# A decoder trunk on one core: x loaded turned and split by features, the value convolution's additions moved into accumulating DMAs, and another order of the DeltaNet groups

## The chip, the cores and the metric

The kernel runs on one core of a Trainium2 chip. The metric is the device time of one execution in microseconds (us); lower is better. The kernel before was timed at a median of 2768.34 us over three runs (2768.11 to 2770.29). One further execution was profiled; it took 2768.12 us, and its trace spans 2766.0 us from the first instruction to the last. The five engines work from queues of their own, each in the order of its queue: PE (TensorE) multiplies matrices, DVE (VectorE) and ACT (ScalarE) work on vectors, POOL (GpSimd) does small vector work and issues DMAs, SP (SyncE) only issues DMAs here.

## The reference

Two layers over 256 tokens of 2048 features. Each has a token mixer and a SwiGLU feed-forward network, each of these behind an RMSNorm and with a residual addition; a last RMSNorm follows.

```
h = x
h = h + gdn_mixer(rmsnorm(h), ...)      # gated DeltaNet, 16 key heads, 32 value heads
h = h + swiglu(rmsnorm(h), ...)
h = h + hgrn2_mixer(rmsnorm(h), ...)
h = h + swiglu(rmsnorm(h), ...)
return rmsnorm(h)
```

All of it is float32. What this change touches is the DeltaNet mixer and the normalization ahead of it:

```
proj = rmsnorm(x) @ w_in                       # k, q, v, z and the gates b, a
qkv  = silu(causal_depthwise_conv(qkv, conv))  # four taps along the tokens
o    = gated_delta_rule_chunked(q, k, v, beta, g)   # chunks of 64 tokens, one 64x64 inverse each
o    = rmsnorm(o) * silu(z)
return o @ w_out
```

rmsnorm divides each token by the root of its mean square. The kernel multiplies the raw x by the norm's weights only and applies the token's factor, called `rstd`, to the products.

## The kernel before

**Weights.** Every weight matrix is streamed once. A "half" is a tile of 128 by 1024 floats (512 KB): SP loads it into one of four buffers `raw`, ACT rounds it to `wh`, DVE forms the rest `wl = raw - wh`, and PE multiplies `wh` with the rounded and the remaining part of the activations (`xt_h`, `xt_l`) and `wl` with the rounded part: three products for one, which keep float32 accuracy. `wh` and `wl` have four buffers each. Results gather in two PSUM tiles called `main`. There are 945 halves.

**Groups.** The halves that make one result tile form a group. In the DeltaNet mixer there is one group for the gates (`ba`, one half, 48 products), and for each of eight head groups (hg) one for keys and queries (k0 to k7, eight halves, 192 products of 256 columns), one for the values (v0 to v7) and one for the output gate (z0 to z7), both of eight halves with 96 products of 512 columns; four output projections o0 to o3 (16 halves each) take the results of two head groups each. `GDN_ORDER` gives the order in which PE works them off; `ba` goes first.

**The start.** `setup` and `start` load the identity and norm weights (`head`) and x in four tiles of 128 tokens by 2 by 512 features (`first0`, `first1`, `x`, `x`), all on the SP queue; ten matmuls of ones warm PE up. PE turns x by 32 transposes into PSUM (`make_xt`), ACT and DVE split what comes out into `xt_h` and `xt_l` (`split_scaled`), and ACT squares and sums x for `rstd` (`sumsq`).

**Between the groups.** When k of a head group is done, `conv_evac` multiplies it by the tokens' factors (`rstd_row`) out of PSUM, `gdn_qk` does the convolution, the decay matrices `dec` and the matrices `nmat`, and `gdn_inverse` inverts: the rows go through DRAM (`n_dram`) into the tile `wide`, 31 pairs of short DVE operations on `u` solve the small blocks, a round trip through DRAM spreads them (`um`, shown as `u`), and PE and ACT join them. When v is done, `gdn_v` copies it into `r`, writes it to DRAM, and reads it back three times shifted by one to three tokens (tile `before`, one buffer); DVE multiplies by the tap's weights and adds to `r`. When z is done, `gdn_o` combines inverse, values and scores and `head_out` gives `ot_h` and `ot_l`, the operands of the output projection. `nmat`, `dec`, `r` and `zs` have two buffers, `wide`, `u` and `before` one.

**Order on the engines.** All operations are first recorded. A planner (`Recorder.plan`) then runs through them with an estimated cost of each and a due time counted back from the products on PE, and fixes every engine's queue; POOL's DMAs are planned with 0.75 us to issue and 6.5 us to land. On the chip each queue runs strictly in that order. Since one helper issues everything, nearly all rows of the profile carry the line L490; groups are told apart by tile.

Of the kernel before, what the change touches and what calls it, by code (L numbers as in the profile page):

```python
# [33 lines left out]
    "k0 k1 k2 k3 v0 v1 z0 z1 v2 k4 z2 k5 v3 z3 k6 v4 o0 k7 v5 v6 z4 o1 z5 z6 v7 z7 o2 o3"  # L34
# [472 lines left out]
class Trunk:  # L507
# [27 lines left out]
    def setup(self):  # L535
# [3 lines left out]
        self.x_at, self.x = self.a["x"], {}  # L539
        head = t([P, P + 64], "head")  # L540
        nc.sync.dma_start(head, self.a["head"])
        nc.ops[-1].lag = 2.4
        self.queue = [nc.ops[-1]]
        self.ident = head[:, 0:P]
        self.norms = head[:, P : P + 64].rearrange("p (n c) -> p n c", n=4)
        self.ones = t([P, P], "ones")
        nc.gpsimd.memset(self.ones, 1.0)
        self.neghalf = t([P, 8], "neghalf")
        nc.gpsimd.memset(self.neghalf, -0.5)
        self.rstd = t([P, 2], "rstd")  # L550
        self.rstdh = t([P, 2], "rstdh")
        self.rstd_row = t([P, T], "rstd_row")
        self.ssp = t([P, 2, 4], "ssp")
        self.ss = t([P, 2], "ss")
        self.junk = t([P, 512], "junk")
        self.vjunk = t([P, 256], "vjunk")
# [3 lines left out]
    def start(self, norm, row):  # L560

        pool = self.nc.pool("first", 1, phase=True)
        for cg in range(4):
            if cg < 2:
                self.x[cg] = self.tile(pool, [P, 2, 512], f"first{cg}")
            else:
                self.x[cg] = self.tile(self.xpool, [P, 2, 512], "x", ordered=True)
            self.nc.sync.dma_start(self.x[cg], self.x_cols(self.x_at, cg))
            self.nc.ops[-1].lag = (2.5, 2.2, 3.0, 3.0)[cg]
            self.nc.edge(self.queue[-1], self.nc.ops[-1])  # L570
            self.queue.append(self.nc.ops[-1])
        warm = self.aux()
        for i in range(10):
            self.nc.tensor.matmul(
                warm[:, (i % 4) * P : (i % 4 + 1) * P], self.ones, self.ones, start=True, stop=True
            )
        for cg in range(4):
            self.make_xt(cg, norm)
        for cg in range(4):
            self.nc.after(self.xt_h[cg])  # L580
            self.sumsq(cg)
        self.nc.close(pool)
        self.make_rstd(row)
# [3 lines left out]
    def stream(self, groups):  # L587
# [10 lines left out]
        def load(n):  # L598
            g, i = flat[n]
            raw = self.tile(self.wraw, [P, 1024], "raw", ordered=True)  # L600
            nc.sync.dma_start(raw, g.halves[i])
            if n == 0:
                nc.ops[-1].lag = 4.2
                nc.edge(self.queue[1], nc.ops[-1])
            h = place("wh", g)
            nc.scalar.activation(h, raw, AF.Copy)
            low = place("wl", g)
            nc.vector.tensor_tensor(out=low, in0=raw, in1=h.bitcast(F32), op=ALU.subtract)
            ready[n] = (h, low)
# [42 lines left out]
    def mm_cols(self, ps, i, wh, wl, n_k, n_f, n_chunks):  # L652

        for k in range(n_k):
            kt = i * n_k + k
            xh, xl = self.operand(kt)
            for f in range(n_f):
                at = (k * n_f + f) * P
                for m, (w, s) in enumerate(((wh, xh), (wh, xl), (wl, xh))):
                    self.nc.tensor.matmul(  # L660
                        ps[:, f // 2, (f % 2) * T : (f % 2 + 1) * T], w[:, at : at + P], s,
                        start=(kt == 0 and m == 0 and f % 2 == 0),
                        stop=(i == 2 * n_chunks - 1 and k == n_k - 1 and m == 2),
                        skip_group_check=True,
                    )
# [616 lines left out]
    def gdn(self, after):  # L1282
# [4 lines left out]
        def gates_end(ps):  # L1287
            self.gdn_gates(ps)
# [472 lines left out]
```

## Time and profile before

| what | value |
|---|---|
| median of three runs | 2768.34 us |
| profiled execution | 2768.12 us |
| its span | 2766.0 us |
| PE busy | 99% of the span |
| weight loads of PE | 84% |
| DVE busy | 69% |
| ACT busy | 52% |
| POOL busy | 9% |
| HBM | 209 GB/s over the span |

The page counts for each engine the time in which one of its instructions runs. A row of a timeline gives the start in us from the span's begin, the duration, engine, line, operation, the tiles written and read, the shapes and the count; in square brackets stands how long the engine was idle before it and what ended that. A matmul's duration is longer than its distance to the next one, as matmuls overlap; the distance is what costs time.

### The profile page before, as it was taken

To read this page: it belongs to the slowest core of one execution; us is meant where nothing else is said; L and a number is where in the kernel's file an instruction comes from. 1 tells how busy PE (TensorE), PEld (TensorE's weight loads), DVE (VectorE), ACT (ScalarE), POOL (GpSimd) and SP (SyncE) were. 2 spreads that over 40 slices of the span, in tenths; PEclk is the share of its full clock that TensorE was granted. 3 is DMA by queue.
4 is the path that set the end of the run, shared out by engine and by line. 5 is a ranking of instruction groups with operands and counts; after the bars stand their busy time and mean duration, and the time that the engine had idled before them with its cause. 6 is when DMAs were issued, how large, how long until landed. Compare 5 with 4: busy or idle time off the path is not lost.

```text
span 2766.0 us, 41091 instructions
## 1 busy us (share of the span) xinstructions
PE 2749.6 (99%) x15662; PEld 2333.5 (84%) x15662; DVE 1899.9 (69%) x2857; ACT 1428.6 (52%) x2010; POOL 251.6 (9%) x370
## 2 busy tenths in 40 slices
PE   9999999999999999999999999999999999999998
PEld 9888888888888888888888989988888888888887
DVE  7787888877766667446675688778657675456764
ACT  6646666565554444344444556556454444344443
POOL 1213222232110000000000100000100000000000
PEclk9999999999999999999999999999999999999999
DMA  7686668687776666676667655555776666766664
GB/s 262 201 282 222 189 213 286 205 276 218 229 254 202 193 194 194 224 223 195 192 191 224 219 163 175 168 166 176 231 258 195 193 193 209 224 208 194 195 200 160
DMA packets 162677, 580.52 MB, mean 210 GB/s; under 512 B 20138, under 2 KB 21306, under 8 KB 162352
## 3 DMA queue, kind: packets, MB, share of 16 engines
q1 hardware_dynamic: 138912, 503.15, 57.0%
q0 software_dynamic: 23280, 73.91, 8.5%
q8 instruction: 122, 2.00, 0.3%
q10 hardware_dynamic: 288, 0.85, 0.1%
q14 instruction: 75, 0.61, 0.1%
HBM read 550.52 MB, written 27.31 MB: 209 GB/s over the span
## 4 chain that ended last, share of the span: by engine, by line
PE 99%; ACT 0%; DVE 0%; issue 0%; DMA 0%; SPq 0%; POOLq 0%; POOL 0%; ACTq 0%
PE main L490 92%; PE aux L490 6%; ACT dec L490 0%; DMA first<-in_x 0%; DVE wl L490 0%; ACT wh L490 0%; DVE utmp L490 0%; SPq L490 0%; DVE pre L490 0%; ACT xt_h L490 0%; DVE u L490 0%; ACT y L490 0%; POOLq L1757 0%; ACT junk L490 0%; DVE xl L490 0%
## 5 line engine op out<-in xcount | busy, mean ns | idle before, releaser
L490 DVE TENSOR_TENSOR wl<-raw,wh 128x1024 fp32r<-128x1024 f32 x945 | 1160.7, 1229 | 755.6 <-ACT wh L490 742.2
L490 ACT ACTIVATE wh<-raw 128x1024 fp32r<-128x1024 f32 x945 | 1000.8, 1060 | 1226.9 <-PE main L490 1126.3
L490 PE MATMUL main<-wh,xt_h 128*128 128x512 f32 x2176 | 849.3, 390 | 0.8 <-ACT wh L490 0.8
L490 PE MATMUL main<-wl,xt_h 128*128 128x512 f32 x2176 | 848.4, 390 | 1.3 <-DVE wl L490 1.3
L490 PE MATMUL main<-wh,xt_l 128*128 128x512 f32 x2176 | 849.5, 390 | 0.0
L490 PEld LDWEIGHTS main<-wl,xt_h 128*128 128x128 f32 x2176 | 408.5, 188 | 85.7 <-DVE wl L490 1.6
L490 PEld LDWEIGHTS main<-wh,xt_h 128*128 128x128 f32 x2176 | 408.5, 188 | 85.0 <-ACT wh L490 1.2
L490 PEld LDWEIGHTS main<-wh,xt_l 128*128 128x128 f32 x2176 | 408.6, 188 | 84.4
L490 PE MATMUL main<-xt_h,wh 128*128 128x256 f32 (+1 forms) x1040 | 290.5, 279 | 0.7 <-ACT wh L490 0.7
L490 PE MATMUL main<-xt_h,wl 128*128 128x256 f32 (+1 forms) x1040 | 290.1, 279 | 1.0 <-DVE wl L490 0.9
L490 PE MATMUL main<-xt_l,wh 128*128 128x256 f32 (+1 forms) x1040 | 290.0, 279 | 0.3 <-DVE xt_l L490 0.3
L490 PE MATMUL main<-wh,htl 128*128 128x512 f32 x664 | 258.6, 389 | 0.0
L490 PE MATMUL main<-wl,hth 128*128 128x512 f32 x664 | 258.3, 389 | 0.0
L490 PE MATMUL main<-wh,hth 128*128 128x512 f32 x664 | 258.3, 389 | 0.0
L490 PEld LDWEIGHTS main<-xt_h,wl 128*128 128x128 f32 (+1 forms) x1040 | 194.5, 187 | 1.5 <-DVE wl L490 1.4
L490 PEld LDWEIGHTS main<-xt_h,wh 128*128 128x128 f32 (+1 forms) x1040 | 194.5, 187 | 1.3 <-ACT wh L490 0.9
L490 PEld LDWEIGHTS main<-xt_l,wh 128*128 128x128 f32 (+1 forms) x1040 | 194.5, 187 | 1.0 <-DVE xt_l L490 0.5
L490 DVE STREAM_TRANSPOSE turned<-h 32x256 f32<-32x256 f32 x352 | 153.5, 436 | 7.2
L490 PE MATMUL main<-wh,ot_l 128*128 128x512 f32 x384 | 151.2, 394 | 0.0
L490 PE MATMUL main<-wh,ot_h 128*128 128x512 f32 x384 | 150.6, 392 | 0.0
L490 PE MATMUL main<-wl,ot_h 128*128 128x512 f32 x384 | 150.5, 392 | 0.0
L490 PEld LDWEIGHTS main<-wh,hth 128*128 128x128 f32 x664 | 124.7, 188 | 25.9
(206 smaller groups left out, 2249.0 us busy)
## 6 DMA issues: line engine op xcount, KB each, us to landing
raw<-in_ffn_gu SPq DMA_DIRECT2D x352, 512.0 KB, 4.7
raw<-in_ffn_d SPq DMA_DIRECT2D x176, 512.0 KB, 4.7
raw<-in_hgrn_in SPq DMA_DIRECT2D x128, 512.0 KB, 4.1
raw<-in_gdn_kq SPq DMA_DIRECT2D x64, 512.0 KB, 5.4
raw<-in_gdn_v SPq DMA_DIRECT2D x64, 512.0 KB, 4.7
raw<-in_gdn_z SPq DMA_DIRECT2D x64, 512.0 KB, 4.9
raw<-in_gdn_out SPq DMA_DIRECT2D x64, 512.0 KB, 5.0
x_home<-x POOLq DMA_DIRECT2D x36, 512.0 KB, 6.7
```

Source lines behind the costliest of these rows:

```text
L490: getattr(getattr(tc.nc, op.eng), op.method)(*args, **kw)
```

## The change

**x turned by the host.** A second copy of x, `x_turned`, comes with the features on the partitions. `start` loads it in eight pieces of 256 KB, two feature blocks each, between the halves of the first group's weights: `head` and the first two pieces on ACT's queue, the others on SP's. The 32 transposes are gone; `split_scaled` reads SBUF where it read PSUM. For `rstd` ACT squares the four tiles in place (128x1024 each), DVE adds them up in four additions, and four matmuls with a column of ones sum over the partitions. There are 11 warm-up matmuls for 10.

**First groups.** `ba` moves behind k0. The first half of k0 is loaded and split in two pieces of 512 columns, and its products run in another order (`wh` on `xt_h`, `wl` on `xt_h`, `wh` on `xt_l`, by feature block). k0 is evacuated by ACT into SBUF and multiplied by `rstd_row` there; the rest of its work is recorded behind the gates.

**Value convolution.** The three `r += before` on DVE become DMAs on POOL's queue that add `before` into `r` in SBUF.

**Order.** v0 goes ahead of k2 and k3, z0 ahead of v1, v3 ahead of z2 and k5, v7 ahead of z6.

```diff
-    "k0 k1 k2 k3 v0 v1 z0 z1 v2 k4 z2 k5 v3 z3 k6 v4 o0 k7 v5 v6 z4 o1 z5 z6 v7 z7 o2 o3"
+    "k0 k1 v0 k2 k3 z0 v1 z1 v2 k4 v3 z2 k5 z3 k6 v4 o0 k7 v5 v6 z4 o1 z5 v7 z6 z7 o2 o3"
...
+        for k in range(2):
+            c = slice(k * 512, (k + 1) * 512)
+            self.in_turn("sync", self.early[0][:, c], first[0][:, c], 3.0)
+            self.in_turn("scalar", *x_piece(k), 3.5 + k)
+        for n in range(1, RAW_BUFS):
+            self.in_turn("sync", self.early[n], first[n], 3.5)
+            self.in_turn("sync", *x_piece(n + 1), 3.5)
+        for j in range(RAW_BUFS + 1, 8):
+            self.in_turn("sync", *x_piece(j), 3.5)
...
-        for cg in range(4):
-            self.make_xt(cg, norm)
+        for cg in range(4):
+            for k in range(4):
+                self.split_scaled(
+                    self.xt_h[cg][:, k, :], self.xt_l[cg][:, k, :], turned[cg][:, k, :],
+                    self.norms[:, norm, 4 * cg + k : 4 * cg + k + 1],
+                )
+        add = lambda out, x: nc.vector.tensor_tensor(out=out, in0=out, in1=x, op=ALU.add)
+        for x in turned:
+            nc.scalar.activation(x, x, AF.Square)
+        for x in turned[1:]:
+            add(turned[0], x)
+        two = turned[0][:, 0:2, :]
+        add(two, turned[0][:, 2:4, :])
...
-    def conv_evac(self, ps):
+    def conv_evac(self, ps, first=False):
...
+        if first:
+            nc.scalar.activation(out, ps, AF.Copy)
+            ps = out
...
             if i < 3:
-                nc.vector.tensor_tensor(out=r, in0=r, in1=x, op=ALU.add)
+                nc.gpsimd.dma_start(r, x, accum_op=ALU.add)
...
-        groups.insert(0, ba)
+        groups.insert(1, ba)
```

More of the change, by code (lines that the diff above doesn't have):

```diff
@@ L555, in setup @@
-        self.junk = t([P, 512], "junk")
-        self.vjunk = t([P, 256], "vjunk")
+        nc.gpsimd.memset(neghalf, -0.5)
+        nc.scalar.dma_start(head, self.a["head"])
+        nc.ops[-1].lag = 2.4
+        self.queue = []
         self.xt_h = [t([P, 4, T], f"xt_h{i}", F32R) for i in range(4)]
         self.xt_l = [t([P, 4, T], f"xt_l{i}", F32R) for i in range(4)]
-    def start(self, norm, row):
-        pool = self.nc.pool("first", 1, phase=True)
-        for cg in range(4):
[L564 to L571, printed above, removed]
+    opening = True
```

129 lines of the change are left out of this document (83 added, 46 removed).

## The prediction

> **What bounds the kernel now.** I read the page first: its engines and its chain, then the view of waits for PE, then stretches.
>
> ```profile
> span 2766.0 us, 41091 instructions
> PE 2749.6 (99%) x15662; PEld 2333.5 (84%) x15662; DVE 1899.9 (69%) x2857; ACT 1428.6 (52%) x2010; POOL 251.6 (9%) x370
> PE 99%; ACT 0%; DVE 0%; issue 0%; DMA 0%; SPq 0%; POOLq 0%; POOL 0%; ACTq 0%
> ```
>
> The chain that ends last is PE's own queue for 99% of the span. A busy PE says little by itself, but that the chain never leaves it does: only PE's work, the time before it can start, and its idle spots can be won. DVE, though 69% busy, is nowhere on the chain.
>
> ```profile
> PE main L490 <- DVE wl L490: 2.2, 2, 1.3
> PE main L490 <- ACT wh L490: 1.5, 2, 0.8
> PE aux L490 <- DMA first<-in_x: 1.3, 1, 1.3
> PE main L490 <- DVE xt_l L490: 0.3, 1, 0.3
> 2000.00:2766.00 766.00, 756.00 (x3352) 626.23 (x3350) 469.97 (x550) 336.64 (x380) 16.44 (x23) 1.00 0.64 203
> ```
>
> The columns of the waits are us in total, times, longest. Of the 16.4 us in which PE idles, 10.0 lie in the last stretch (766.0 less 756.0), behind the last product, which the change does not touch; 1.3 and 0.3 are in the start and 1.1 ahead of the first matmul; 3.7 are four waits for `wh` and `wl`, which stand here with what ACT did just then:
>
> ```profile
> 302.62 0.39 PE L490 MATMUL main<-xt_h,wh 128*128 128x256 f32 x1 [0.69 <-ACT wh L490]
> 304.06 0.39 PE L490 MATMUL main<-xt_h,wl 128*128 128x256 f32 x1 [0.94 <-DVE wl L490]
> 391.18 0.50 PE L490 MATMUL main<-wh,xt_h 128*128 128x512 f32 x1 [0.79 <-ACT wh L490]
> 392.98 0.50 PE L490 MATMUL main<-wl,xt_h 128*128 128x512 f32 x1 [1.29 <-DVE wl L490]
> ...
> 381.53 5.86 ACT L490 ACTIVATE dec<-g_row,shift 128x64 f32<-128x64 f32 x24 [0.16 <-PE aux L490]
> 387.40 1.28 ACT L490 ACT_TABLE_LOAD   x1
> 388.70 1.49 ACT L490 ACTIVATE dec<-dec 128x1536 f32<-128x1536 f32 x1
> 390.10 3.88 ACT L490 ACTIVATE wh<-raw 128x1024 fp32r<-128x1024 f32 x4
> ```
>
> ACT's queue has 8.6 us of `dec` in one piece (381.53 to 390.10). Four `wh` follow back to back, so the weights had landed: PE had eaten what was split ahead. So two stalls of the DeltaNet part come from the planner's order on ACT, not from DVE's load.
>
> **The change: the start.** Rows of the timeline, the chain's row for the first 40 us (the DMA piece), and a stretch with k1's products:
>
> ```profile
> 1.07 4.63 PE L490 MATMUL aux<-ones 128*128 128x128 f32 x20 [1.07 <-POOL ones L490]
> 5.50 1.08 PE L490 MATMUL aux<-head,first 128*128 128x128 f32 x8
> 6.18 0.84 ACT L490 ACTIVATE xt_h<-aux,head 128x256 fp32r<-128x256 f32 x2 [2.05 <-PE aux L490]
> 7.06 0.88 DVE L490 SCALAR_TENSOR_TENSOR xt_l<-aux,head,xt_h 128x256 fp32r<-128x256 f32 x2 [7.06 <-ACT xt_h L490]
> 8.77 0.36 PE L490 MATMUL main<-xt_h,wh 128*64 128x256 f32 x1
> 16.88 0.28 PE L490 MATMUL main<-xt_h,wh 128*128 128x256 f32 x1
> 34.12 0.42 DVE L490 TENSOR_TENSOR u<-main,rstd_row 64x256 f32<-64x256 f32 x1
> 39.14 0.28 PE L490 MATMUL main<-xt_h,wh 128*128 128x256 f32 x1
> ...
> 2.21 5.67 DMA first<-in_x
> ...
> 39.14:61.37 22.23, 22.04 (x195) 21.84 (x193) 1.22 (x1) 0.00 (x0) 1.00 0.70 220
> L490 DVE TENSOR_TENSOR wl<-raw,wh 128x1024 fp32r<-128x1024 f32 x945 | 1160.7, 1229 | 755.6 <-ACT wh L490 742.2
> L490 ACT ACTIVATE wh<-raw 128x1024 fp32r<-128x1024 f32 x945 | 1000.8, 1060 | 1226.9 <-PE main L490 1126.3
> ```
>
> Now the first product starts at 8.77, k0 at 16.88, k1 at 39.14. A k group of 192 products takes 22.23 us, so a product 0.116. Both kernels have 48 + 192 = 240 products before k1, 27.8 us; 30.4 lie between 8.77 and 39.14, and the 2.6 more are the transposes behind the first product (16 at 1.08/8 = 0.135, 2.2) and waits.
>
> After the change:
> - *First product.* Eleven matmuls of ones are 22 rows at 4.63/20 = 0.23, so PE is free at about 6.1. What the product needs is `head`, one x piece and half a weight tile: 608 KB, as many as `head` and the first x tile now, which PE had by 5.5; ACT then rounds the weights (half of 1060 ns and a little, 0.6) and x (0.4): between 5.9, where the weights land first, and 6.6. I take 6.1, when PE is free anyway.
> - *The second half.* Its weights are the last of 1632 KB (two weight tiles, `head`, two x pieces); now the second x tile is the last of as many (96 + 3 x 512) and lands at 2.21 + 5.67 = 7.9. Then 1.06 on ACT and 1.23 on DVE: `wl` at 10.3. PE wants it at 6.1 + 26 x 0.116 = 9.1, since only the first half has the other order: a wait of 1.2 (0.3 to 2.5 with the landing).
> - *The fifth half* is the last of 4704 KB, as four x pieces stand ahead of it. From 608 KB at 5.3 to 1632 at 7.9 the queues bring 394 KB per us: it lands at 15.7, `wl` is there at 18.1, PE comes at 18.4. Nothing, by a hair.
> - k1 then starts at 6.1 + 27.8 + 1.2 + 0.2 (four small matmuls for the sums, two for `rstd_row`) = 35.3: **3.8 us earlier** (2.0 to 4.9 by the ends above).
>
> A rule that speaks against the 6.1: the Trainium skill, "TensorE: Matmul & The Clock Gate", Part 1, says that PE runs at half its clock until a window of about 3.4 us was busy, and that the window runs freely. The pace of 0.23 and then 0.135 in the rows agrees with a turn at about 5.6. By the page it could come up to 3.4 us later, and the sum would lose some 1.2 us.
>
> *Edits that cost nothing.* The gates move behind k0, to 35.3; their first step waits now for `rstd_row` until 34.12, so they lose 1 us, and k0's own evacuation, no longer waiting, is earlier. ACT gets a copy of some 1.06 for k0 and four squares of 1024 columns for eight of 512, DVE four additions (three as long as a `wl`, one of half the size, some 4.3 us): hidden beside k0's 22 us, in which PE needs 2.78 us a half, ACT 1.9 (1.06 and 0.84) and DVE 2.1 (1.23 and 0.88). If that cover went, the start's gain would shrink by as much.
>
> **The change: the accumulating DMAs and the order.** The view of the tile `before`, and from the DMA list the write of `r`, the nearest transfer out of SBUF:
>
> ```profile
> L490 POOL DMA_DIRECT2D before<-v_rows x24: 704/716/736, 143.2 to 730.7; - x24
> L490 DVE TENSOR_TENSOR r<-r,before x24: 1212/1218/1653, 155.2 to 741.6; 128x1024 f32<-128x1024 f32 x24
> DMA to landing us min/median/max: 3.9/5.8/10.5
> ...
> v_rows<-r POOLq DMA_DIRECT2D x8, 512.0 KB, 6.1
> ```
>
> DVE loses 24 x 1.22 = 29 us, none of it on the chain: worth 0. POOL gains 24 issues of 0.72, 17 us on 252, hidden by its 91% of idle time. But each landing now stands between one tap and the next: `before` has one buffer, so its next load waits on POOL for the accumulation, and POOL's work behind it (masks of `dec`, the clearing of `u`, writes to `n_dram`) waits too; at the last tap ACT's queue, `wh` in it, stops at the Silu of `r` if the planner's 6.5 us were too few. No accumulation is in the trace. From below its time A is 3.9, the shortest landing of the same size; from above 10.5, the longest. I take 6.1, the row that also leaves SBUF.
>
> Where does that come to PE? Values are due long before their output projection except at the end: v7's must be through `gdn_o` when o3 reaches head group 7. Rows of that stretch, taps first:
>
> ```profile
> 715.50 1.22 DVE L490 TENSOR_TENSOR before<-before,taps 128x1024 f32<-128x1024 f32 x1
> 719.73 0.70 POOL L490 DMA_DIRECT2D before<-v_rows  x1 [2.16 <-DVE so L490]
> 726.89 1.21 DVE L490 TENSOR_TENSOR before<-before,taps 128x1024 f32<-128x1024 f32 x1
> 730.67 0.73 POOL L490 DMA_DIRECT2D before<-v_rows  x1 [5.41 <-DVE r L490]
> 738.22 1.22 DVE L490 TENSOR_TENSOR before<-before,taps 128x1024 f32<-128x1024 f32 x1
> 744.45 1.06 ACT L490 ACTIVATE r<-r 128x1024 f32<-128x1024 f32 x1
> ...
> 779.12 1.40 DVE L490 SCALAR_TENSOR_TENSOR ot_l<-aux,gdn_hn,ot_h 128x512 fp32r<-128x512 f32 x2
> ...
> 782.99 0.39 PE L490 MATMUL main<-wh,ot_h 128*128 128x512 f32 x1
> ```
>
> The first `ot_l` is done at 779.8 and o3 asks at 782.99: 3.2 us to spare, the tightest place. From a tap's multiplication to the next step take 4.2, 3.8 and 6.2 us, 14.2 in all; after, 1.4 + A each. The new order puts v7 one z group earlier (as many columns as a k group, 22.2 us), and the start moves o3 up by 3.8. To spare: 3.2 - 3.8 + 22.2 + 14.2 - 4.2 - 3A = 31.6 - 3A, which is 13 us at A = 6.1 and nothing at 10.5. So the DMAs cost 0 here, and the moved v7 pays for them.
>
> The Trainium skill, "Collectives: The Full Stack", "Why ReduceScatter is half of AllGather", speaks against cheap accumulation: the add itself is free, but two sources are read through one ring, which halves the rate. No run here shows it yet; as an estimate, 512 KB at the 394 KB per us above take 1.3 us, so doubling gives A = 7.4. The sum would be the same with 9 us to spare, and the rival on A below a little likelier.
>
> The other moves (v0, z0, v3) change which vector work meets which; the two stalls on ACT may stay, go or double. I keep their 3.7 us.
>
> **Sum**, against the profiled execution's 2768.12 (0.2 below the median): 2768.1 - 3.8 = **2764.3 us**, 0.15% below the median. About 0.2%, 5.5 us, is what a measurement of this kernel can tell from no change, so the likeliest case lies just inside it; its own range is 2762 to 2768 (start -4.9 to -2.0, stalls halved or doubled).
>
> **The rivals.**
> - *The stalls go as well.* A new order on ACT splits `dec` from the `wh` behind it, and 29 us less on DVE lets `wl` run ahead: -3.7 more, 2760.6. For it: only two of eight head groups stall now. Against: nothing in the change touches ACT's 8.6 us.
> - *The accumulation is slow and o3 waits* (the other side). From A = 10.5 each us more costs PE three; past 11.8 the start's gain is spent, past 13.6 the kernel is over 0.2% slower; at 14 it is 2764.3 + 10.5 = 2774.8. For it: one `before` under load took 10.5, and an accumulation moves more than a copy. Against: the median is 5.8.
> - *The change doesn't do what it says at the start*: the weights still land too late. Second half 2.5 and first product 6.6 (or the first products at the warm-up's pace, 1.2): gain 2.0, 2766.1. For it: the queues bring all they can in the first 10 us in either kernel. Against: the first product needs 608 KB where it needed 1120 (`head`, an x tile, the gates' weights).
>
> **Chances.** Forecast 0.50, stalls gone 0.25, slow accumulation 0.15, small start 0.10. Faster by over 0.2%: the 0.25 and 0.06 of the forecast's lower edge, 0.31. Slower by over 0.2%: 0.12 of the 0.15 and 0.05 for a doubled set of stalls with a long A, 0.17. Within: 0.52. The range goes from the stalls gone with the best start (2760.6 - 1.1, rounded to 2759) to A = 14.7 (2764.3 + 12.6 = 2777).
>
> **What would show it.** Right: first product at 6 to 6.6, a wait for `wl` of about 1 us near 9, k1 at 35 to 36; no `make_xt` rows before it; accumulations landing in 6 to 8 us; no PE wait at o3's third half. Wrong: PE waits for `wh` behind an ACT Silu of `r`; landings over 10 us; raw loads held up so that several halves in the DeltaNet part wait; o3 waiting for `ot_h`.

## The result, and the profile after

The changed kernel takes 2772.99 us, the median of 22 runs (2769.11 to 2777.22), beside 2769.23 us for the kernel before on the same chip (22 runs, 2767.58 to 2770.92): a ratio of 1.0015, with a 95% interval of 1.0009 to 1.0022. It is slower by 0.15%, 3.8 us, where 2764.3 us had been forecast. Its profiled execution took 2777.15 us, 4.2 above its median, so the rows below show more stalls than a median run has. A second traced execution, in which every engine worked through the same instructions in the same order (the first run under "What in the start costs" below), took 2771.37 us; some of its numbers stand beside the first.

The page of the changed kernel, its engines and the chain that ended last:

```profile
span 2775.4 us, 41040 instructions
PE 2749.1 (99%) x15640; PEld 2331.0 (84%) x15640; DVE 1881.0 (68%) x2837; ACT 1427.0 (51%) x2000; POOL 279.5 (10%) x394
...
PE 93%; DMA 3%; issue 1%; DVE 1%; POOL 0%; ACT 0%; SPq 0%; POOLq 0%; DVEq 0%; ACTq 0%
```

The engines' busy shares have hardly moved; the chain has. PE held 99% of it, now 93%, and transfers hold 3%. The view of waits for PE (us in total, times, longest) says where it left PE:

```profile
PE main L490 <- DVE wl L490: 7.4, 3, 3.4
PE main L490 <- ACT xt_h L490: 3.3, 2, 2.0
PE aux L490 <- DVE inv L490: 2.2, 2, 1.9
PE aux L490 <- DVE dec L490: 1.7, 1, 1.7
```

Against the kernel before, whose waits came to 6.4 us in all, three things are new: `xt_h` at the start, longer single waits for `wl`, and waits of PE's small products for `inv` and `dec`, links in the DeltaNet's chain that never reached PE before.

**The start.** The timeline of the changed kernel, with the row of its stretches for 13.57 to 16.98 us below (stretch, its length, PE's busy time and rows, granted clock, DMA share, GB/s):

```profile
1.25 0.46 ACTq L490 DMA_DIRECT2D head<-in_head  x1
1.39 1.25 POOL L490 DMA_DIRECT2D x<-in_x  x2 [0.28 <-issue]
6.50 0.33 SPq L490 DMA_DIRECT2D first<-in_x_turned  x1
7.61 0.51 ACT L490 ACTIVATE xt_h<-first,head 128x256 fp32r<-128x256 f32 x1 [0.64 <-DMA head<-in_head]
8.17 0.74 PE L490 MATMUL main<-xt_h,wh 128*128 128x256 f32 x4 [2.04 <-ACT xt_h L490]
12.43 0.38 PE L490 MATMUL main<-xt_h,wh 128*128 128x256 f32 x1 [1.25 <-ACT xt_h L490]
13.68 0.58 PE L490 MATMUL main<-xt_l,wh 128*128 128x256 f32 x1 [0.87 <-DVE xt_l L490]
40.59 0.28 PE L490 MATMUL main<-xt_h,wh 128*128 128x256 f32 x1
...
13.57:16.98 3.41, 3.30 (x15) 0.50 1.03 403
```

The first product starts at 8.17, 0.6 earlier than before, and not at 6.1: `head`, 96 KB and second on ACT's queue, is issued at 1.25 and lands at 7.5; in the kernel before it went out first, at 0.82, and landed at 2.8. Two loads of `x`, 512 KB each, leave on POOL from 1.39 on, into the middle of the start's transfers; before, these buffers held the start's own x, and the loads went out from 27.48 on (the first one's row stands in the second fence of the gates below). SP's next transfer goes out only at 6.50, and the planner has put the fifth weight tile (9.39) ahead of the last four pieces of x (9.76 to 16.70), not behind them. PE then idles twice more, and for one window of 3.41 us it gets half its clock: 15 products where full clock would give some 29 (3.41/0.116). k1's first product is at 40.59, 1.5 us later than the 39.14 before; in the second execution it is at 39.57, 0.4 later.

**The gates.** Rows of the timeline around the sums of squares and the row of ACT's `dec` from the view of that tile (duration in ns, then the first and the last start of eight head groups), of the changed kernel first and then of the kernel before:

```profile
37.88 0.16 DVE L490 TENSOR_SCALAR ss<-aux 128x2 f32<-128x2 f32 x1 [1.04 <-PE aux L490]
...
43.37 0.42 DVE L490 TENSOR_TENSOR u<-main,rstd_row 64x256 f32<-64x256 f32 x1
...
L490 ACT ACTIVATE dec<-dec x8: 1488/1491/1493, 88.1 to 638.6; 128x1536 f32<-128x1536 f32 x8
```

```profile
27.48 0.54 POOL L490 DMA_DIRECT2D x<-in_x  x1 [0.46 <-ACT neg L490]
...
28.02 0.17 DVE L490 TENSOR_SCALAR ss<-ss 128x2 f32<-128x2 f32 x1
...
L490 ACT ACTIVATE dec<-dec x8: 1489/1491/1492, 76.2 to 625.2; 128x1536 f32<-128x1536 f32 x8
```

The sums, due on PE after four squares and four additions, are 9.9 us later (37.88 for 28.02), the gates' first step 9.3 (43.37 for 34.12), and the first `dec` 11.9 us later, though k1 itself is only 1.5 late. The last piece of x has landed at 22.4, ACT's last three squares run from 27.5 to 30.4, DVE's additions end at 34.6, and the products of the sums stand on PE at 36.89, behind k0 and part of the gates' own products. In this kernel the DeltaNet's chain does not make this up: the last `dec` is 13.4 late. In another plan of the same work it does (under "The plan's number" below).

**The DeltaNet part.** Four of the stalls of the changed kernel, and the three stretches at half clock behind them:

```profile
243.01 1.23 DVE L490 TENSOR_TENSOR r<-r,taps 128x1024 f32<-128x1024 f32 x1 [5.30 <-DMA taps<-in_gdn_conv_v]
248.46 0.39 PE L490 MATMUL main<-xt_h,wl 128*128 128x256 f32 x1 [3.36 <-DVE wl L490]
305.94 1.22 DVE L490 TENSOR_TENSOR before<-before,taps 128x1024 f32<-128x1024 f32 x1 [2.88 <-DMA before<-v_rows]
312.24 0.50 PE L490 MATMUL main<-wl,xt_h 128*128 128x512 f32 x1 [2.68 <-DVE wl L490]
363.06 0.24 PE L490 MATMUL aux<-inv,nmat 32*32 32x32 f32 x2 [1.90 <-DVE inv L490]
585.71 0.45 PE L490 MATMUL aux<-inv,nmat 32*32 32x32 f32 x32 [1.74 <-DVE dec L490]
...
249.09:252.50 3.41, 3.41 (x18) 0.50 0.82 221
365.14:368.55 3.41, 3.41 (x10) 0.50 0.50 177
587.01:590.42 3.41, 3.41 (x10) 0.50 0.59 191
```

At 243 DVE has waited 5.3 us for a load of `taps`, with `wl` behind it in its queue; PE runs dry. Behind PE's idle times of 1.7 to 3.4 us stand windows of half clock, up to 1.7 us each (half of 3.41); the wait of 2.68 us at 312 drew none (in the second execution a wait of 2.54 there drew one). The windows lie on one grid: from the first at 13.57, the others start 235.52, 351.57 and 573.44 later, which is 69, 103 and 168 times 3.413. The load of `taps` was issued at 232.78 and took 10.2 us to land; it stands in POOL's queue behind a load of `before` (222.72) for which POOL had waited 6.5 us, until an accumulation landed. Such waits show in the view of the tile `before` of the changed kernel, with the accumulation's row of the DMA list (KB, median us to landing):

```profile
L490 POOL DMA_DIRECT2D r<-before x24: 882/916/977, 161.4 to 740.2; - x24
its engine sat idle before it (us, times) until:
  DMA r<-before: 72.7, 18
...
r<-before POOLq DMA_DIRECT2D x24, 512.0 KB, 7.1
```

An accumulation lands in 7.1 us at the median (5.0 to 10.4 over the 24), and POOL stands 18 times, 72.7 us in all, behind such a landing, because the next `before` goes into the same buffer. Everything POOL issues waits with it. Not every stall goes back to that: the one at 363 follows a load of `wide` that took 11.2 us to land, with no accumulation on its chain.

**A gain elsewhere.** The same 2040 products of the HGRN part, before and then after, as stretches:

```profile
1563.46:1908.26 344.80, 344.80 (x2843) 1.00 0.54 172
```

```profile
1578.28:1917.93 339.65, 339.65 (x2842) 1.00 0.56 176
```

Neither idles, yet the changed kernel is 5.15 us shorter there. In the trace of before, 831 products of 128x256 follow each other at 120 ns, in that of after at 113 or 114.

**Where the time went.** The two spans differ by 9.45 us (2775.44 and 2765.99). k1 starts 1.5 later; from there to the end of the last output projection of the DeltaNet part the changed kernel takes 13.7 us more (798.4 for 784.8), of which 7.7 are idle time of PE (11.4 for 3.7) and up to 5.1 the three windows at half clock; behind it, it takes 5.7 less. In the second execution, nearer to the median, these are 0.4 later, 8.9 more (9.3 us of idle time and one window) and 5.7 less. So nearly all of the loss lies in the DeltaNet part behind k1.

### The profile page after: what moved, and what is told of

It reads as the page before. It is cut to its first block, busy times and chain, and to the rows that moved or that the text cites. A ratio compares the mean times of both kernels' runs of the same rounds, so it can differ in the third digit from the quotient of the medians.

```text
span 2775.4 us, 41040 instructions
## 1 busy us (share of the span) xinstructions
PE 2749.1 (99%) x15640; PEld 2331.0 (84%) x15640; DVE 1881.0 (68%) x2837; ACT 1427.0 (51%) x2000; POOL 279.5 (10%) x394
## 4 chain that ended last, share of the span: by engine, by line
PE 93%; DMA 3%; issue 1%; DVE 1%; POOL 0%; ACT 0%; SPq 0%; POOLq 0%; DVEq 0%; ACTq 0%
PE main L490 88%; PE aux L490 6%; DMA before<-v_rows 1%; DVE wl L490 0%; DMA wide<-n_dram 0%; DMA taps<-in_gdn_conv_v 0%; DMA r<-before 0%; DMA raw<-in_gdn_kq 0%; ACT dec L490 0%; ACT wh L490 0%; DVE u L490 0%; SPq L490 0%; DVE before L490 0%; POOL u L490 0%; DVE utmp L490 0%
## 5 line engine op out<-in xcount | busy, mean ns | idle before, releaser
L490 DVE TENSOR_TENSOR wl<-raw,wh 128x1024 fp32r<-128x1024 f32 (+1 forms) x946 | 1163.6, 1231 | 772.0 <-ACT wh L490 761.8
L490 ACT ACTIVATE wh<-raw 128x1024 fp32r<-128x1024 f32 (+1 forms) x946 | 1000.8, 1059 | 1244.4 <-PE main L490 1115.6
L490 PEld LDWEIGHTS main<-wl,hth 128*128 128x128 f32 x664 | 124.6, 188 | 26.0
```

Of the source, the lines that this page charges most:

```text
L490: getattr(getattr(tc.nc, op.eng), op.method)(*args, **kw)
```

## The experiments

The change was taken apart into start, placement of the constants, order of the groups, and accumulations. All times are medians with the kernel before beside them on the same chip (2768.7 to 2769.6 us).

**Placement alone.** The kernel before, with only the constants' sizes and order of the changed kernel:

```diff
+        neghalf = t([P, 72], "neghalf")      # was 8 wide, and behind head and ones
+        rstd, rstdh, ssp, ss                 # now ahead of head
-        self.vjunk = t([P, 256], "vjunk")
+        self.vjunk = t([P, 320], "vjunk")[:, 0:256]
```

> The kernel before, with the small constant tiles in the sizes and the order of the changed kernel (one of 72 columns for 8, one of 320 for 256), nothing else. Theory: these tiles shift all buffers behind them by 512 bytes, and that alone makes the 831 products of the HGRN stage that take 120 ns take 113. Then that stage is 5.1 to 5.4 us shorter and the median is 2763 to 2764.5. Rival: the stage is shorter because the planner's order there differs; then the products at 120 ns stay and the time is 2769.

Measured: 2764.21 us, ratio 0.9981 (0.9971 to 0.9990): faster than either kernel, and all of it in HGRN. To find what does it, the pads were tried alone (`neghalf` 72 wide, `neghalf` 136 wide, `vjunk` 320 wide, both pads), and the order alone.

> The kernel before with one constant, `neghalf`, 72 columns wide instead of 8, and nothing else: all tiles laid out behind it move by 256 bytes in each partition, where the changed kernel moves them by 512 and orders the constants differently. Theory (the slow pace of 831 products in the HGRN part, 120 ns for 113, hangs on where the tiles lie, and 256 bytes also leave the bad place): HGRN 5.4 us shorter, 2764 (2762.8 to 2765.5). Rival (it takes the whole 512 bytes, or the other order): 2769.3 (2768 to 2771), with 120 ns as before; something between if only some of the tiles leave it.

> The kernel before with `neghalf` 136 columns wide instead of 8, nothing else: the tiles behind it move by the 512 bytes that the changed kernel's constants take, without its other order of the constants. Theory (512 bytes are enough, since 256 did nothing): products of 128x256 in HGRN at 113 ns, 5.4 us shorter, 2764 (2762.8 to 2765.5). Rival (the place of the constants themselves decides, `rstd_row` and the like, by their order): 2768.7 (2767.8 to 2770.6), HGRN as before.

> The kernel before with its constants laid out in the changed kernel's order (the small ones ahead of `head`), but without the wider `neghalf` and `vjunk`. Theory (the order decides, since 512 bytes behind the constants did nothing): HGRN 5.4 us shorter, 2764 (2762.8 to 2765.5), no products at 120 ns there. Rival (the pads decide, the order does nothing): 2768.7, with 831 products at 120 ns.

> The kernel before with both pads, `neghalf` 72 and `vjunk` 320 columns wide, in the old order. Theory (order decides): 2768.7 with 120 ns in HGRN. Rival (256 bytes on either side of the constants decide): 2764.

> The kernel before with `vjunk` 320 columns wide alone. Theory (order decides): 2768.7 with 120 ns in HGRN. Rival (the 256 bytes ahead of the start's tiles decide): 2764.

Measured: the pads did nothing (2768.32, ratio 0.9997; 2768.84, 1.0000; 2769.54 and 2769.52, both 1.0001; all intervals hold 1). The order alone gave 2763.81 us, ratio 0.9981 (0.9970 to 0.9992). The HGRN stretch with `neghalf` 136 wide, and with the order alone:

```profile
1566.32:1911.12 344.80, 344.80 (x2843) 1.00 0.53 172
```

```profile
1563.73:1903.38 339.65, 339.65 (x2842) 1.00 0.55 176
```

So it is neither the 512 bytes nor the pads, but the place of the small constants, `head`, `ones` or `rstd_row`; all engines run the same instructions in the same order. Which of these tiles it is, and why PE's pace hangs on it, no run shows.

**Order alone, additions alone, both.** In the kernel before, one line each:

```diff
-    "k0 k1 k2 k3 v0 v1 z0 z1 v2 k4 z2 k5 v3 z3 k6 v4 o0 k7 v5 v6 z4 o1 z5 z6 v7 z7 o2 o3"
+    "k0 k1 v0 k2 k3 z0 v1 z1 v2 k4 v3 z2 k5 z3 k6 v4 o0 k7 v5 v6 z4 o1 z5 v7 z6 z7 o2 o3"
...
-                nc.vector.tensor_tensor(out=r, in0=r, in1=x, op=ALU.add)
+                nc.gpsimd.dma_start(r, x, accum_op=ALU.add)
```

> The kernel before with nothing but the new order of the DeltaNet groups; additions on DVE, the old start, the old placement in SBUF. Theory (the late stalls of the second run, which had this order and DVE additions, come from the order): that run stood 8.9 us above the kernel before; taking back 5.4 us of placement and 1.5 us of a late start leaves 8.9 + 5.4 - 1.5 = 12.8 us for the order, so 2769.2 + 12.8 = 2782 (2778 to 2785), with a wait of 4 to 5 us of PE's aux products for `zs` of DVE just after 790 and several stalls with `dec` between 580 and 680. Rival (those stalls needed the new start's timing as well; the order alone is as good as the old one): 2768 to 2771, and no wait over 1.5 us in the DeltaNet part.

> The kernel before with the accumulating DMAs alone (old order, old start). Theory of the held POOL queue: new stalls of PE in the DeltaNet part and windows at half clock, 4 to 12 us slower than before, and o3 waits in addition, as v7 isn't moved ahead: 3A - 10 less 3 to spare, 8 us at A = 7. Rival: the accumulations are harmless by themselves and the order is to blame: within 3 us of 2769.

> The kernel before with the accumulating DMAs and the new order together; old start, old placement. Alone the accumulations cost 14.4 us (2783.65) and the order 9.8 us (2779.07). Theory (each puts stalls of its own into the DeltaNet part, so they add): 2769.3 + 24.2 = 2793.5 (2788 to 2799), with 15 us and more of PE's idle time. Rival (the order is the one that goes with the accumulations: values are asked for earlier, so a long landing is late for nobody): about the changed kernel without its placement, 2773.0 + 5.1 = 2778.1 less what the new start costs there (0 to 6.5): 2771.6 to 2778.

Measured: the order alone 2779.07 us, ratio 1.0037 (1.0024 to 1.0050), as its theory had it; the accumulations alone 2783.65, 1.0052 (1.0033 to 1.0070), more than the 4 to 12 us of its theory; both together 2770.61, 1.0008 (0.9999 to 1.0017). Alone they cost 9.8 and 14.4 us, together 1.1: for the pair its rival's mechanism held, a microsecond below the rival's range, and not the sum of 24. What sorts these runs at their longest wait are two rows whose later number, the last start, belongs to the last head group: its values are ready behind `r<-r,pwqk`, its inverse behind `inv<-u`, and o3 needs both. Accumulations alone, with PE's wait at o3:

```profile
L490 ACT ACTIVATE r<-r,pwqk x32: 487/494/512, 201.1 to 781.0; 128x256 f32<-128x256 f32 x32
...
L490 DVE STREAM_TRANSPOSE inv<-u x32: 422/434/437, 196.1 to 757.3; 32x256 f32<-32x256 f32 x32
...
PE aux L490 <- DVE zs L490: 5.5, 2, 4.8
```

Order alone, with the same wait in the timeline:

```profile
L490 ACT ACTIVATE r<-r,pwqk x32: 492/494/512, 176.7 to 730.6; 128x256 f32<-128x256 f32 x32
...
L490 DVE STREAM_TRANSPOSE inv<-u x32: 424/434/437, 197.1 to 765.7; 32x256 f32<-32x256 f32 x32
...
794.43 0.45 PE L490 MATMUL aux<-head,zs 128*128 128x128 f32 x1 [4.35 <-DVE zs L490]
```

Both, with POOL's idle time behind accumulations:

```profile
L490 ACT ACTIVATE r<-r,pwqk x32: 490/492/511, 168.3 to 743.0; 128x256 f32<-128x256 f32 x32
...
L490 DVE STREAM_TRANSPOSE inv<-u x32: 423/434/436, 190.3 to 744.3; 32x256 f32<-32x256 f32 x32
...
  DMA r<-before: 23.8, 7
```

With the accumulations alone the values are late, 781.0; with the order alone they are early, 730.6, and the inverse is late, 765.7; PE stands still for 4 to 5 us at o3 in both, and behind each wait stand two windows of half clock (800.45 to 807.28 and 794.05 to 800.88). The rest of what they lose lies in shorter stalls ahead of o3; both traces are the slowest of their runs (2789.65 and 2784.04 us) and show more of these than the medians have. Together they meet at 743.0 and 744.3, and PE does not wait. Before it was 748.9 and 740.0. So the two parts mend each other: v7 is worked earlier, which makes up for the landings, and DVE, rid of the additions, gets the inverse done. That DVE's additions are what delays the inverse in the second run is read from this, not measured apart, and it is not all: with the accumulations alone DVE has no additions either, and the inverse is at 757.3. Along the way POOL stood behind accumulations for 23.8 us here, where the changed kernel has 72.7.

**The start alone, and the change without its start.** First the changed kernel with DVE additions, and then also with the old order:

> The changed kernel with the additions of the value convolution on DVE again. Theory: the accumulating DMAs hold POOL's queue, taps and loads behind them come late, and DVE and ACT stop with the weights behind. Then of the 9.6 us that PE idles between product 240 and 2400 at most 5 stay, at most one of the three windows at half clock after 40 us stays, and the median is 2766 to 2769. Rival: the new order of the groups makes the stalls; then idle time and windows stay and the time is within 2 us of 2773.

> As the run before, without the hold: the new start as the change has it, the new placement, DVE additions and the old order. Theory: placement -5.4, start +1.5, stalls as before: 2765.3 (2763.5 to 2767). Rival (the new start's later k1 and the lone stalls upset the old order too): 2770 and more. Against the run with the hold it prices the two early loads at the end of the kernel.

The first took 2778.13 us, ratio 1.0030 (1.0019 to 1.0041), outside both its theory and its rival. It holds start, placement and order, and PE waits 4.8 us for `zs` at o3 as with the order alone. The second, start and placement, took 2770.72 us, ratio 1.0005 (0.9995 to 1.0014); placement alone took 2764.21, so this start with the queues planned for it costs 6.5 us, and the rival held. Then the opposite, the change with everything but its start:

> The changed kernel without its start, everything else as the change has it: accumulating DMAs, new order, placement, 6.5 us in the planner. Theory (the start is the part of the change that costs; accumulations with their order cost 1.1 us, placement takes 5.4): 2769.3 + 1.1 - 5.4 = 2765 (2763.5 to 2766.5), so 4 us faster than before. Rival (each plan draws stalls of its own, as the run with 9.0 us in the plan did): 2767.5 to 2772. The plan here is the one of accumulations with the order, since placement is not in it, so this run also tells whether stalls repeat with the plan.

Measured: 2765.25 us, ratio 0.9985 (0.9976 to 0.9995), as the theory had it. Its queues are those of accumulations with the order, instruction by instruction, and its waits of PE for `wl` and `wh` are the same to 0.1 us (2.9 and 1.2 in total): so far the same plan draws the same stalls. Its row of `dec`:

```profile
L490 ACT ACTIVATE dec<-dec x8: 1488/1491/1492, 78.2 to 627.5; 128x1536 f32<-128x1536 f32 x8
```

The changed kernel, 2772.99 us, differs from it by the start alone, with the queues that the planner makes of it: 7.7 us, or 7.2 if each is taken against the kernel before beside it. The first `dec` is at 78.2 with the old start and at 88.1 with the new one, the last at 627.5 and at 638.6.

**What in the start costs.** The two early loads of `x` were to be held back, first by an edge in the planner, which put no wait on the chip, so that they still went out at 1.40 us:

> The changed kernel, but the two loads of x for the first output projection (POOL, 512 KB each, issued at 1.39 and 2.09 us there) wait for the last split of the start. Theory: they took the bandwidth of the start. Then the first product is at 6.1 to 6.8 us instead of 8.17, the second half's weights land near 8.5 instead of 10.9, no window at half clock follows in the first 20 us, and k1 starts at 36 to 37 us instead of 40.59: the median falls by some 4 us, to 2769. Rival: the SP queue itself holds x back (eight transfers in flight, and the fifth half's weights, waiting for a buffer, ahead of the fifth x piece); then k1 stays within 1 us of 40.6 and the time at 2773.

Measured: 2773.08 us, ratio 1.0012 (1.0003 to 1.0022). The order on every queue is that of the changed kernel, so it tells nothing about the loads; it is the changed kernel once more. Then with a real one, eight columns of each tile written by DVE from the start's last result:

```diff
+        if self.x_at is self.a["x"] and cg < 2:
+            self.nc.vector.tensor_tensor(
+                out=self.x[cg][:, 0, 0:8], in0=self.xt_l[3][:, 3, 0:8].bitcast(F32),
+                in1=self.xt_l[3][:, 3, 0:8].bitcast(F32), op=ALU.subtract)
         self.nc.gpsimd.dma_start(self.x[cg], self.x_cols(self.x_at, cg))
```

> The changed kernel, but the two early loads of `x` on POOL are really held: DVE first writes eight columns of each tile from the last low part of the start, so that the loads can't start before about 25 us. Theory (the two loads of 512 KB spoil the start): raw c1, x pieces and raw1 land 2 to 3 us earlier, k1 starts at 37 to 38 instead of 40.6, and the time falls by as much, to 2769 to 2771. Rival (SP's queue is what is late: its sixth transfer waits for the first landing, and weight tiles 4 and 5 stand ahead of the x pieces): k1 moves by less than 1 us and the time stays at 2772 to 2774.

> The changed kernel with DVE additions, the old order, and the two early loads of `x` really held as in the run before: what is left of the change is the new start and the new placement of the tiles in SBUF. Theory: placement -5.4 us, start between +0.5 (if the loads were not the cause) and -3 (if they were), the old order's stalls stay at about 3.7 us: 2761 to 2764.5. Rival (a start that ends at another time upsets the old order's match of vector work with PE too, as it did with the new order): stalls of 6 us and more, 2767 to 2775.

Measured: the changed kernel with the hold 2770.35 us, ratio 1.0005 (0.9996 to 1.0015), and the start with placement alone 2769.40, 0.9998 (0.9989 to 1.0008). k1's first product in the first of these:

```profile
37.93 0.28 PE L490 MATMUL main<-xt_h,wh 128*128 128x256 f32 x1
```

37.93 for 40.59, or for the 39.57 of the second execution: the early loads cost 1.6 to 2.7 us at k1, and the median falls by 2.6, as the theory had it. The first product stays at 8.12, so what delays that is not these loads. With the old order and DVE additions k1 comes 1.2 earlier with the hold (38.10 for 39.32) and the median falls by 1.3 (2770.72 to 2769.40). Each ratio is known to about 0.1%, 2.7 us, so at the end these prices are not clear of the noise; at k1 it is 1.2 to 2.7. But in the second run the rival held: it still stands 5.2 us above placement alone, although its k1, at 38.10, is a microsecond earlier than before. So most of what this start costs here is paid behind k1, in the DeltaNet part. The last hand on the start, with `head` first on ACT's queue and all x pieces ahead of the fifth weight tile on SP's, and 9.0 us in the plan as in the run below:

```diff
+        else:
+            self.nc.edge(self.head_load, op)          # ACT: head before the x pieces
...
+                if n < 8:
+                    nc.edge(self.queue[-1], nc.ops[-1])   # SP: weights behind the x pieces
```

> The changed kernel with 9.0 us for an accumulation in the planner and a start whose loads come in the turn that the prediction assumed: the two early loads of `x` held as before, `head` ahead of the x piece on ACT's queue, and on SP's queue all x pieces ahead of the fifth weight tile. Theory (the start fell short through these three): first product at 6.1 to 7, no wait over 1.5 us and no half-clock window in the first 240 products, k1 at 35.3 to 36.5, that is 2.6 to 3.8 us before the kernel before, and the time 2767.2 - 3.1 to 4.3 = 2763 to 2764. Rival (SP's and ACT's queues hold back whatever the turn, since a further load waits for the first landing): k1 at 37.5 to 39 as with the hold alone, the time 2765 to 2767.

Measured: 2768.15 us, ratio 0.9998 (0.9988 to 1.0007), k1 at 40.79. Neither theory had this. Its rows:

```profile
8.29 1.06 ACT L490 ACTIVATE wh<-raw 128x1024 fp32r<-128x1024 f32 x1 [1.42 <-DMA raw<-in_gdn_kq]
9.26 0.89 ACT L490 ACTIVATE xt_h<-first,head 128x256 fp32r<-128x256 f32 x2
9.80 1.22 PE L490 MATMUL main<-xt_h,wh 128*128 128x256 f32 x4 [3.88 <-ACT xt_h L490]
```

The planner, told of other loads, put the second weight tile's rounding, whose load ends at 8.29, ahead of the first `xt_h`, whose data was there by 6.5. PE waited 3.88 us, and half clock followed. What the right turn of the loads is worth was therefore not measured. It did bring `head` in at 5.3 and the first piece of x at 6.5, so even then the first product could not have started at 6.1.

**The plan's number for an accumulation.** In the changed kernel, the planner is told 9.0 us to landing for 6.5; then the same with the old start:

```diff
                 nc.gpsimd.dma_start(r, x, accum_op=ALU.add)
+                nc.ops[-1].lag = 9.0
```

> The changed kernel with one number of its planner changed: an accumulating DMA is counted with 9.0 us to its landing, where the planner counted 6.5 and the trace showed a median of 7.1 and up to 10.4. Nothing is added or left out; instructions are only put in another order on their queues. Theory (the stalls of 240 to 600 us come from a plan that has the landings too early, so that other work queues behind them on POOL and ACT): PE's idle time between k1 and the end of the DeltaNet part falls from 11.4 to 6 us or less, half-clock windows from three to one or none, and the time to 2766 to 2769. Rival (the landings' lateness matters little, and any new order of the plan draws another set of stalls): idle 8 to 15 us, 2771 to 2778.

> The kernel before with four parts of the rest: the changed kernel's placement of the constants, the accumulating DMAs, the new order, and 9.0 us for an accumulation in the planner. What is left out of the changed kernel is its start. Theory (the start costs, and the rest is sound once the plan has the landings right): accumulations with the order stood 1.1 us above the kernel before; placement takes 5.4, and the plan with 9.0 took 7.1 us of PE's losses after k1 in the changed kernel but can here take no more than the 4 or so of stalls and half clock that are left: 2769.3 + 1.1 - 5.4 = 2765 without help from the plan, 2761 with: 2760 to 2766, faster than either kernel. Rival (every new plan draws its own stalls, the good one with 9.0 was luck): 2767 to 2775, with a wait of over 3 us or a half-clock window somewhere in the DeltaNet part.

Measured: 2767.21 us, ratio 0.9991 (0.9982 to 1.0000), 5.8 us less than the changed kernel, with POOL behind landings for 39.7 us instead of 72.7:

```profile
  DMA r<-before: 39.7, 10
```

That bore the theory out, until the same number without the start gave 2769.11 us, ratio 1.0003 (0.9994 to 1.0013), 3.9 us more than with 6.5, as the rival had it. So the number decides which stalls a plan gets, and 9.0 is not simply the better one. That the stalls of the changed kernel hang on the plan is shown: the same instructions in another order idle PE for 5.0 us behind k1 instead of 11.4. That a truer number mends them in general is not.

These two runs differ by the start alone as well, and here the new start costs nothing that the measurement can tell: 2767.21, 2.3 below the kernel before beside it, for 2769.11, 0.4 above, with each ratio known to about 0.1%. The gates are as late as in the changed kernel (first step at 42.45, for 34.67 with the old start), and yet the chain catches up. The rows of `dec`, new start first:

```profile
L490 ACT ACTIVATE dec<-dec x8: 1488/1490/1492, 87.2 to 627.3; 128x1536 f32<-128x1536 f32 x8
L490 ACT ACTIVATE dec<-dec x8: 1488/1488/1492, 78.6 to 629.4; 128x1536 f32<-128x1536 f32 x8
```

The first `dec` is 8.6 us late and the last 2.1 early. So the 6.5 and 7.7 us are what the start costs in the plans made with 6.5 us, not a price of the start or of its late gates as such.

## Why the prediction was wrong

Two terms of the sum failed: the start's gain of 3.8 us, which did not come, and the stalls, kept at 3.7 us, which came to 11.4 with half clock behind them and make up most of the loss. A third, a gain of 5 us, was not in the sum.

**The start** failed first. "First product... I take 6.1": it was 8.17. The step counted bytes in the order of the queues and took what had to land as 608 KB; but several transfers run side by side, so a small early one lands late (`head`, 96 KB, 6.3 us after its issue), and `head` stood second on ACT's queue. The step that took the loads of the start to be all that moves was wrong too: freed buffers let POOL's two `x` loads go from 1.39 on, which the hold priced at 1.2 to 2.7 us at k1. The start of k1, put at 35.3, was 40.59, 5.3 us off, and 39.57 in the second execution. The wait for `wl` (1.2 forecast) became three waits for `xt_h` and `xt_l`. That the copy, the squares and the additions hide beside k0 held: PE has no wait from 13.68 to k1.

**The gates** were a misreading. "They lose 1 us" was worked out against `rstd_row` at 34.12, as if that stayed; but with this start `rstd_row` needs sums over squares of the whole of x, and the products of these sums stand on PE behind k0. The gates' first step came 9.3 us later, and head group 0's `dec` 11.9. The text held that k0's evacuation would be earlier; the copy is (37.92 for 40.14), but the multiplication by `rstd_row` stands at 43.71. What this slip cost stays open. In the plans made with 6.5 us the start costs 6.5 to 7.7, most of it behind k1, and the late gates are a likely part of that; with 9.0 in the plan they are as late and the new start costs nothing that shows. No run left the gates in front.

**"The DMAs cost 0 here"** held at o3 and failed in reach. A was taken as 6.1, within 3.9 to 10.5, and measured 7.1, within 5.0 to 10.4; the Trainium skill, "Collectives: The Full Stack", "Why ReduceScatter is half of AllGather", had led to an estimate of 7.4, near the measured median. That is luck: the plain write of `r`, whose 6.1 the estimate started from, takes 7.4 in the changed kernel's trace, and the plain loads of `before` 6.8, so no run here shows that an accumulation takes longer than a copy. That the moved v7 pays for them is borne out: 1.1 us together. Without the move, in the old order and with the old start, the reckoning gives 3.2 + 14.2 - 4.2 - 3 x 7.1 = -8.1; PE waited 4.8 there, the right sign at half the size (PE itself came to o3 later by then, through other stalls). But 31.6 - 3A followed v7's taps alone. With v7 early, the last head group's inverse decides at o3, which the text did not follow; at 759.6 in the changed kernel (740.0 before) it was not late: `zs` was done at 791.4, and PE asked for it at 793.98. And no cost was looked for earlier in the part: POOL's hold reached `taps`, DVE and so `wl` at 243, a chain the text named without a price when it said that POOL's work behind the landing waits too.

**"I keep their 3.7 us"** is the step that cost most: PE idles 11.4 us between k1 and the end of the DeltaNet part in the profiled run (9.3 in the second execution), with windows of half clock on top. The text kept the term as a middle between stalls that go and stalls that double; but the planner makes new queues when the work changes, and the stalls come with the queues. Runs with the same queues show stalls at the same places (the pads, the placement, and the change without its start beside accumulations with the order), though their length can differ: 3.36 and 0.76 us ahead of 248.5 and 244.8 in the two executions of the changed kernel. Runs with other queues show others, and one number of the planner moved the time by 5.8 us. Why one order of the queues draws more stalls than another is not shown. The rival that the stalls would go, at 0.25, had them on the wrong side.

**A term was missing.** The constants' new order is in the diff and was passed over; it gave back some 5 us in HGRN (5.1 by the run with the placement alone). By that sum the changed kernel would have been about 9 us slower than before without it, not 3.8. That the measured time lies within 2759 to 2777 us is luck: the upper end was put there for a slow accumulation, and this gain hid more than half of the loss.

**The clock.** The rule of the Trainium skill, "TensorE: Matmul & The Clock Gate", Part 1, was used for the warm-up alone, where it was to cost some 1.2 us. The trace agrees with its free-running window of about 3.4 us (3.41, all four on one grid), but what counted was that the windows come back. At the start PE's warm-up products end at 6.1 and the first product comes at 8.2, with more waits behind it: all eight traces with the new start have one or two windows of half clock between 7.3 and 17 us, of the twelve with the old start one has. And windows come back in the middle of the kernel. The Trainium skill, "TensorE: Matmul & The Clock Gate", "Why this matters for your kernels", warns of idle gaps above some 3 us; here 1.74 and 1.90 us were followed by a window each, and the measurement decides. Even the old queues can draw a window: with `neghalf` 136 wide, where nothing stands in another order than before, two waits that the kernel before has as well (0.79 and 1.29 there) were followed by one.

```profile
392.51 0.49 PE L490 MATMUL main<-wh,xt_h 128*128 128x512 f32 x1 [0.81 <-ACT wh L490]
394.28 0.50 PE L490 MATMUL main<-wl,xt_h 128*128 128x512 f32 x1 [1.28 <-DVE wl L490]
...
395.54:398.95 3.41, 3.41 (x23) 0.50 0.82 256
```

In the profiled run of before the same two waits drew none. How a stall falls into the grid may decide; no run shows it. So a stall's price is its idle time and, at times, up to 1.7 us more for each window behind it (one here, two at o3 with the order alone).

Of the rivals, none was the one that came. "The change doesn't do what it says at the start" was nearest, at 0.10, and still gave a gain of 2.0 us; the slow accumulation, the one on the right side of zero, did not occur.

## What to carry to other kernels

When a step is moved, follow what it feeds, not only the engine that it leaves: here the sums of squares moved 10 us back, and the gates and the eight head groups' chain with them, though PE itself began earlier. Where a planner fixes the order, price a change together with the plan made for it: with one number of the planner changed, the same late chain caught up and the change's loss was gone. Parts of a change can be worth far more or less together than alone: additions on DMAs and the order made for them cost 14.4 and 9.8 us apart and 1.1 together. And a freed buffer is also a load that may start at once, in the middle of what one tried to hasten; the best version here keeps the start of before and takes from the change only the order of its constants (2763.8 us, ratio 0.9981).

## What the runs showed of the hardware that was not expected

- The place of a few small constants in SBUF changes the pace of products that the engines issue in the same order: 831 products in HGRN at 120 ns or at 113 to 114, 5.15 us in the stretch shown. Shifts of 256 and 512 bytes by pads did nothing; the reason is open.
- Idle times of PE of 1.74, 1.90 and 3.36 us, and in one run two waits of 0.81 and 1.28 within 3.4 us, were followed by 3.41 us at a granted clock of 0.50, all windows of the changed kernel's trace on one grid; a wait of 2.68 us was not followed by one.
- An accumulating DMA of 512 KB within SBUF lands in 5.0 to 10.4 us, beside the stream of weights. Its issue shows as 0.92 us on POOL where that of a plain load of `before` shows as 0.72, but POOL's next instruction can start 0.57 us after it (214.55 and 215.12).
